# A mean over rows, loaded in blocks of 256 rows: which partition receives which pair of rows

## The chip, the cores and the metric

The kernel runs on one core of one Trainium2 chip. The metric is the device time of one execution, in microseconds. The kernel before takes 1244.01 us, the median of three runs (1243.89, 1244.03 and 1244.01).

## The reference: what is computed

The input is `x`, fp32, of shape (64, 256, 8192): 16,384 rows of 8,192 numbers, 536.9 MB. The output is the mean of each row.

```python
def reference(x):
    return np.mean(x, axis=2)
```

## The kernel before

Everything is bound together by one large stream of loads from HBM into the on-chip buffer memory (SBUF, 128 partitions).

**The blocks.** The 16,384 rows are cut into 64 lots of 256 rows. The first 63 of them (`NB` = 63) are the blocks. A block is 8 MiB. Each of the 128 partitions receives one *pair* of rows, that is two rows that lie behind each other in HBM, 64 KB in one piece. In the kernel before, partition p gets pair p of the block (`blocks`, L39), so a block is read as one contiguous stretch, cut into 128 pieces.

**The buffers and the load queue.** There are three buffers of 8 MiB (`bufs`, `NBUF` = 3). All loads are issued by SP, in order, on one hardware queue, and the chip's DMA engines, sixteen for this core, carry them out. The first block is issued as two loads (8 KB of each partition at L114, the other 56 KB at L115), so that a first semaphore comes early; blocks 1 and 2 follow at L117. Then a loop (L118 to L123) runs over the other 60 blocks: SP waits at L120 until the buffer is free, and issues the next load into it at L121. The loop picks its block with a register as index.

**The sums.** VectorE (DVE) waits for each block and adds up both rows of all partitions with one instruction (L163, `tensor_reduce` of 128 x 16384). Its result goes to two columns of `res`, and the instruction's end frees the buffer. The last three blocks are handled at L173 and, the very last, in two halves by the helper at L145.

**The last 256 rows** are loaded in smaller pieces so that little is left to do after the last byte: 128 rows, one per partition (`one`, L125), three groups of 32 rows with a quarter row per partition (L127), and a fourth group in four narrow pieces (L129). DVE and ScalarE (ACT) add them up as they land.

**The way out.** `res` holds, in partition p and columns 2g and 2g + 1, the sums of the two rows of partition p of block g. TensorE multiplies `res` by a diagonal matrix that holds 1/8192 (L226), which turns it: `turn[0]` and `turn[1]` have a block per partition and the 128 pairs as columns. ACT copies the two into `turned`, one into the even columns and one into the odd (L207), so that a partition of `turned` holds the 256 means of a block in the order of the output. SP stores that with one DMA (L133). The last 256 means go through `row` and leave by L135.

## Time and profile before

| | |
|---|---|
| median of three runs | 1244.01 us |
| the profiled execution's own time | 1243.67 us |
| its span, first to last instruction | 1242.4 us |
| DVE busy | 1085.4 us (87%) |
| DMA queue, share of sixteen engines' span | 99.8% |
| moved | 536.94 MB, 432 GB/s over the span |
| one sum of a block (L163) | 17.22 us, 60 times |
| issue of a block's load by SP (L121) | 0.33 us, 60 times |
| from issue to landing of a block's load | 40.3 us, two loads in the queue |

The page of the profile gives busy time by engine, then the span in forty slices, the DMA queue, the chain of work that ended last, and the groups of instructions. "L163" is line 163 of the kernel. The share of the DMA queue says how much of the sixteen engines' time was taken by packets. Each packet here is one contiguous piece of a load, as large as 64 KB.

### The profile page before, as it was taken

Reading aid. Unit: us, or ns where it says so; the run is one execution under the profiler, and the core shown is the slowest. Engines: PE = TensorE matmul, PEld = TensorE weight load, DVE = VectorE, ACT = ScalarE, POOL = GpSimd, SP = SyncE. Lnnn points to the kernel's source line nnn. Section 1 sums busy time; section 2 is a strip of 40 time slices with the busy share of each in tenths; the row PEclk is TensorE's granted clock in tenths of the full one; section 3 lists DMA queues with packets and bytes.
Section 4 is the critical chain, followed back from the end, with each engine's and each line's share of the span. In section 5 each row is a group of like instructions: output and inputs, shape, how many; then the busy total and the mean of one; then the engine's idle time right before and its main releaser. Section 6 shows DMA issues by size and latency. Waiting matters only on the chain. (4 is left out here: it accounts for less than half of the span.)

```text
span 1242.4 us, 656 instructions
## 1 busy us (share of the span) xinstructions
PE 3.3 (0%) x20; PEld 1.4 (0%) x20; DVE 1085.4 (87%) x78; ACT 3.7 (0%) x8; POOL 1.6 (0%) x11
## 2 busy tenths in 40 slices
PE   0000000000000000000000000000000000000001
PEld 0000000000000000000000000000000000000000
DVE  2898988989889898898898988989889898898988
ACT  0000000000000000000000000000000000000000
POOL 0000000000000000000000000000000000000000
DMA  9999999999999999999999999999999999999998
GB/s 405 439 439 439 439 411 433 439 439 439 439 439 420 424 439 439 439 439 439 426 418 439 439 439 439 439 426 418 439 439 439 439 439 433 414 437 439 439 439 373
DMA packets 10442, 536.94 MB, mean 432 GB/s; under 512 B 1162, under 2 KB 1482, under 8 KB 1738
## 3 DMA queue, kind: packets, MB, share of 16 engines
q1 hardware_dynamic: 10442, 536.94, 99.8%
HBM read 536.87 MB, written 0.07 MB: 432 GB/s over the span
## 5 line engine op out<-in xcount | busy, mean ns | idle before, releaser
L163 DVE TENSOR_REDUCE res<-buf 128x16384 f32 x60 | 1033.2, 17220 | 146.9 <-DVEq L162 146.9
L173 DVE TENSOR_REDUCE res<-buf 128x2 f32<-128x16384 f32 x2 | 34.4, 17221 | 4.0 <-DMA buf<-in_x_dram 4.0
L145 DVE CUSTOM_DVE_ANT_0 buf<-buf 128x4096 f32<-128x4096 f32 (+2 forms) x7 | 17.2, 2485 | 4.2 <-DMA buf<-in_x_dram 4.2
L226 PE MATMUL turn<-diag,res 128*63 128x128 f32 x4 | 1.1, 428 | 1229.6 <-DVE res L145 1229.6
L207 ACT ACTIVATE turned<-turn 63x128 f32<-63x128 f32 x2 | 0.6, 281 | 1228.4 <-PE turn L226 1228.3
L226 PEld LDWEIGHTS turn<-diag,res 128*63 128x63 f32 x4 | 0.7, 217 | 1229.6 <-issue 1229.6
L235 PE MATMUL psum<-sel,part 128*1 128x32 f32 x14 | 1.6, 225 | 3.9 <-DVE part L145 3.1
L215 ACT ACTIVATE buf<-buf 128x896 f32<-128x896 f32 (+1 forms) x2 | 1.4, 709 | 7.9 <-DMA buf<-in_x_dram 7.8
L207 ACT ACT_TABLE_LOAD x1 | 1.3, 1283 | 0.7 <-PEq L262 0.7
L90 POOL TENSOR_SCALAR_AFFINE_SELECT sel<-sel 128x32 f32<-128x32 f32 x4 | 0.9, 213 | 0.7 <-POOL sel L87 0.2
L196 DVE TENSOR_REDUCE part<-buf 128x1 f32<-128x256 f32 x1 | 0.4, 419 | 0.3 <-DMA buf<-in_x_dram 0.3
L235 PEld LDWEIGHTS psum<-sel,part 128*1 128x1 f32 x14 | 0.6, 80 | 5.3 <-DVE part L145 3.9
L230 PE MATMUL psum<-diag,res 128*1 128x128 f32 x2 | 0.6, 394 | 4.1 <-DVE res L145 4.1
L200 DVE COPY row<-psum 1x32 f32<-1x32 f32 x1 | 0.2, 178 | 0.4 <-PE psum L235 0.4
L215 ACT ACTIVATION_READ_ACCUMULATOR buf<-buf 128x1 f32 x2 | 0.4, 186 | 0.0
L217 ACT ACTIVATE row<-psum 1x224 f32<-1x224 f32 x1 | 0.3, 330 | 0.0
L145 DVE DVE_READ_ACCUMULATOR2_ANT part<- 128x1 f32 x4 | 0.3, 81 | 0.0
L101 POOL TENSOR_SCALAR_AFFINE_SELECT diag<-diag 128x128 f32<-128x128 f32 x1 | 0.3, 295 | 0.1
L145 DVE DVE_READ_ACCUMULATOR2_ANT res<- 128x1 f32 x3 | 0.2, 83 | 0.0
L99 POOL MEMSET diag<- 128x128 f32 x1 | 0.2, 206 | 0.0
L87 POOL MEMSET sel<- 128x32 f32 x1 | 0.1, 125 | 0.3 <-POOLq L262 0.3
L262 POOL MEMSET const-bfloat16-1.0<- 128x1 bf16 x1 | 0.1, 102 | 0.0
(4 smaller groups left out, 0.4 us busy)
## 6 DMA issues: line engine op xcount, KB each, us to landing
buf<-in_x_dram SPq DMA_DIRECT2D x1, 7168.0 KB, 21.2
buf<-in_x_dram SPq DMA_DIRECT2D x4, 1024.0 KB, 34.1
buf<-in_x_dram SPq DMA_DIRECT2D x1, 4096.0 KB, 31.1
buf<-in_x_dram SPq DMA_DIRECT2D x62, 40.3
buf<-in_x_dram SPq DMA_DIRECT2D x1, 448.0 KB, 37.7
buf<-in_x_dram SPq DMA_DIRECT2D x1, 288.0 KB, 37.9
buf<-in_x_dram SPq DMA_DIRECT2D x1, 160.0 KB, 37.9
buf<-in_x_dram SPq DMA_DIRECT2D x1, 128.0 KB, 37.8
```

The lines of the kernel that those rows point to most:

```text
L90: eng.affine_select(out=sel[:], in_=sel[:], compare_op=mybir.AluOpType.not_equal, fill=inv, base=-q, pattern=[[-PER, G]], channel_multipli ...
L101: eng.affine_select(out=diag[:], in_=diag[:], compare_op=mybir.AluOpType.not_equal, fill=inv, base=0, pattern=[[-1, P]], channel_multiplier=1,
L145: eng.tensor_tensor_reduce(ap[:, 0:n], ap[:, 0:n], ap[:, n : 2 * n], scale=1.0, scalar=0.0, op0=ADD, op1=ADD, accum_out=to,).then_inc(done, 1)
L163: eng.tensor_reduce(early[:, bass.ds(i, 1), b, :], bufs[b][:].rearrange("p (j l) -> p j l", j=2), X, ADD,).then_inc(free_sems[b], 1)
L173: eng.tensor_reduce(res[:, 2 * g : 2 * g + 2], bufs[b][:].rearrange("p (j l) -> p j l", j=2), X, ADD,).then_inc(free_sems[0] if b == 0 els ...
L196: eng.tensor_reduce(part[:, PER + 2 : PER + 3], group(PER - 1)[:, a:z], X, ADD).then_inc(part_d, 1)
L207: eng.activation(turned[:, j : 2 * P : 2], turn[j][:, 0:P], COPY).then_inc(copy_sem, 1)
L215: eng.activation(ap, ap, COPY, accum_out=part[:, to : to + 1]).then_inc(part_a, 1)
L217: eng.activation(row[:, 0 : 2 * P - G], psum[0][:, 0 : 2 * P - G], COPY).then_inc(row_sem, 1)
L226: eng.matmul(turn[j][:, 0:P], res[:, j : 2 * NB : 2], diag[:], start=True, stop=True).then_inc(turn_sem, 1)
L230: eng.matmul(psum[0][:, 0:P], res[:, 2 * NB : 2 * NB + 1], diag[:], start=True, stop=True)
L235: return eng.matmul(dst, part[:, n : n + 1], sel[:], start=start, stop=stop)
```

## The change

The list of blocks is cut by another pattern. Within a block of 128 pairs, partition 8e + j now receives pair 16j + e, with e from 0 to 15 and j from 0 to 7. The pieces stay 64 KB, each contiguous, and a load still names all 128 partitions in order. What differs is the source side of the load: before, 128 steps of 64 KB; after, 16 outer steps (e) of 64 KB, and inside each 8 steps (j) of 1 MiB. The index of the block becomes the first dimension of the pattern. Since the partitions now hold the pairs in another order, ACT's copy into `turned` reads its 128 columns as 16 times 8 and writes them as 8 times 16, which puts the means back in the order of the output. The loads of the last 256 rows and everything on DVE and TensorE stay as they were.

```diff
+    RUN = 16
-    blocks = flat[0:M, :].rearrange("(g p j) l -> p g (j l)", p=P, j=2)
+    blocks = flat[0:M, :].rearrange("(g j e t) l -> g e j (t l)", g=NB, e=RUN, t=2)
...
-        later = blocks[:, NBUF:, :].rearrange("p (i b) w -> b p i w", b=NBUF)
-        eng.dma_start(bufs[0][:, 0:FIRST], blocks[:, 0, 0:FIRST]).then_inc(first_sem, 16)
-        eng.dma_start(bufs[0][:, FIRST:], blocks[:, 0, FIRST:]).then_inc(in_sems[0], 16)
+        later = blocks[NBUF:].rearrange("(i b) e j w -> b i e j w", b=NBUF)
+        eng.dma_start(bufs[0][:, 0:FIRST], blocks[0][:, :, 0:FIRST]).then_inc(first_sem, 16)
+        eng.dma_start(bufs[0][:, FIRST:], blocks[0][:, :, FIRST:]).then_inc(in_sems[0], 16)
         for b in range(1, NBUF):
-            eng.dma_start(bufs[b][:], blocks[:, b, :]).then_inc(in_sems[b], 16)
+            eng.dma_start(bufs[b][:], blocks[b]).then_inc(in_sems[b], 16)
         with eng.Fori(0, ROUNDS) as i:
             for b in range(NBUF):
                 eng.wait_ge(free_sems[b], 1).then_inc(free_sems[b], -1)
-                eng.dma_start(bufs[b][:], later[b][:, bass.ds(i, 1), :]).then_inc(
+                eng.dma_start(bufs[b][:], later[b][bass.ds(i, 1)]).then_inc(
                     in_sems[b], 16
                 )
...
-            eng.activation(turned[:, j : 2 * P : 2], turn[j][:, 0:P], COPY).then_inc(
-                copy_sem, 1
-            )
+            eng.activation(
+                turned[:, j : 2 * P : 2].rearrange("g (j e) -> g e j", e=RUN),
+                turn[j][:, 0:P].rearrange("g (e j) -> g e j", e=RUN),
+                COPY,
+            ).then_inc(copy_sem, 1)
```

## The prediction

> **What bounds the kernel now.** I read the page first: the share of the DMA queue, beside the busy share of the fullest engine.

> ```profile
> span 1242.4 us, 656 instructions
> PE 3.3 (0%) x20; PEld 1.4 (0%) x20; DVE 1085.4 (87%) x78; ACT 3.7 (0%) x8; POOL 1.6 (0%) x11
> ...
> DMA  9999999999999999999999999999999999999998
> ...
> q1 hardware_dynamic: 10442, 536.94, 99.8%
> ```

> The sixteen DMA engines are full from end to end; DVE has 13% to spare. The stretches view says the same without the start and the tail (columns: stretch, its length, busy time of PE, weight loads, DVE, ACT, POOL, clock, DMA share, GB/s):

> ```profile
> 31.00:620.00 589.00, 0.00 (x0) 0.00 (x0) 525.42 (x31) 0.00 (x0) 0.00 (x0) 1.00 1.00 434
> 620.00:1180.00 560.00, 0.00 (x0) 0.00 (x0) 499.25 (x29) 0.00 (x0) 0.00 (x0) 1.00 1.00 434
> ```

> 434 GB/s in both, with a DMA share of 1.00. Next the waits, of the engines and of SP's queue:

> ```profile
> DVE res L163 <- DVEq L162: 146.9, 60, 22.6
> ```

> ```profile
> SPq L120 <- SPq L120: 1140.5, 60, 37.1
> SPq L133 <- ACT turned L207: 28.1, 1, 28.1
> SPq L135 <- DVE row L200: 9.8, 1, 9.8
> ```

> DVE waits at every block (22.6 us for the first, then about 2.1 us each), so it follows the loads. SP waits about 19 us for each free buffer, and yet each load then stands 40.3 us between issue and landing, twice a block's time: a second load is always queued ahead of it.

> The trace's own record of single packets says what "full" means. Of 7,936 pieces of 64 KB, 7,485 took exactly 2,418 ns; the shortest took 2,415 ns and the mean is 2,419.0. That is 27.1 GB/s for an engine, and sixteen of them are the 434 GB/s above. Pieces of 32 KB take 1,213 ns and pieces of 8 KB 309 ns: from 32 to 64 KB, 32,768 bytes more for 1,205 ns, 27.2 GB/s again. So a piece moves at a fixed rate of its engine's path, no engine slows another, and nothing in it varies as a shared memory's answer would.

> **The change part by part.** The sum is made against the profiled execution's 1243.67 us (0.03% below the median 1244.01).

> *What it can save.* The aim is sixteen engines reading neighbours. If every piece fell to the shortest seen, that is 63 blocks x 8 pieces per engine x (2,419.0 - 2,415) ns = 2.0 us, 0.16%. The start holds no more: the 128 first pieces of 8 KB averaged 344 ns over a usual 309, 8 x 35 ns = 0.3 us per engine. Neighbouring reads are already in this trace: the three quarter-row groups (L127) read 1 MiB stretches with all sixteen engines in them, and their 384 pieces all took 309 ns, the price of that size. I take a gain of 0.

> *SP's issues.* 60 times L121, 0.33 us each, two loads at L117 and two for the first block, all with a source pattern of one dimension more. Bounds: unchanged, or twice as long, 0.33 us more each. SP waits 19 us ahead of each and the queue holds another load, so 0. For the first load there is no cover: it is issued at 0.75 us for 0.42 us, so at most 0.4 us. I take 0.

> *ACT's two copies* (L207), 281 ns each, written in steps of 32 numbers instead of 2. Bounds: same, or three times as long, 1.1 us more for both. They end at 1231.0, SP's store L133 follows (0.37 us), and SP then waits 9.8 us at L135 for `row`. Cost 0; without that cover, 1.1 us. ACT's next work, L215, waits 7.8 us for a landing behind them. TensorE, POOL and the loads of the last 256 rows issue what they did.

> *DVE's* sums are the same 60 x 17.22 us. They lie beside the loads as long as a load takes longer than 17.22 us.

> *How a load is cut among the engines.* This is the term that decides. A load names 128 partitions; its source had 128 outer steps and now has 16, with 8 inside. As I read it, the new pattern hands one outer step, and with it eight neighbouring partitions (8e to 8e + 7), to each engine. Whether the engine had those partitions before, the profile doesn't show, since it has no engine or partition for a packet. If before the engines were dealt partitions so that each had an entry to SBUF of its own, eight neighbours each may put two engines at one entry, at the same moment, while other entries stand idle. Bounds: nothing, if the 27.1 GB/s is the engine's own limit; and if it is the entry's, two engines share it and each piece takes 2 x 2,418 ns. The nearest rows for both ends are the piece itself and the block cadence: DVE's sums at L163 start at 22.6 us and, 59 blocks later, at 1162.9, so 19.33 us a block. I take the upper end. The rows that lean that way: the rate is the same for 8 KB pieces and 64 KB pieces, near ones and far ones, and all sixteen engines hold it within 0.1%, which is how sixteen separate, exactly full paths look. If it is a path's limit, sharing is paid in full.

> [...]

> *How long they meet.* [...] The packet record has the sixteen engines starting their first piece within 0.45 us of each other. All pairs must end for a block to end, so the pair with the smallest lead counts; I take 0.1 us, which is 0.2 us a block. Nothing in the trace makes a lead grow.

> The sum: 63 blocks x 19.33 us = 1217.8 us more, less 63 x 0.2 = 12.6 us: 1243.67 + 1217.8 - 12.6 = 2448.9. I predict 2449 us. DVE would then be busy 44% (1085.4 of 2449) and SP's waits twice as long.

> **The rivals.**

> *A. Not slower: the limit is in the engine, not at the entry.* Or the cut stays as it was. Then each piece keeps its 2,418 ns wherever it is written, 8 x 2.42 = 19.3 us a block, and the time is 1243.7 us with a bound of 2 us below. For it: the same uniform rate, which an engine's own limit explains as well. It decides as soon as a piece written beside its neighbour takes 2.42 us and not more. Against it: that the change touches the very shape by which the load is cut.

> *B. The pairs meet at first and drift apart.* [...] Then the first blocks take 38.7 us and later ones 19.3. With the crossing done on average halfway, the loss is half: 1243.7 + 609 = 1853 us; quick drift would give 1300, slow drift 2400. [...] Against it: pieces that agree to 1 ns in 2,418 point to a very even treatment of the engines.

> *C. HBM is slower for neighbours.* The engines are in step, 64 KB apart. The only slow pieces of the trace are those of the first load, 344 ns on average instead of 309. As a bound, 11% on the 1218 us of blocks, 134 us; a third of it gives about 1290 us. Against it stand the 384 pieces at 309 ns.

> *D. Faster by more than 0.2%.* It needs pieces below the shortest of 7,936, or the 2.2 us outside the packets.

> **How the numbers follow.** 0.2%, 2.5 us, is about what a measurement of this kernel can tell from no change. I give the forecast 0.40: the rows allow a limit of the path or of the engine, and of these the path with its full pairing is a little likelier, given that the shape by which the load is cut changes. B gets 0.27, the same limit with an uneven split. A gets 0.25, all of it within 0.2%. C gets 0.06 and D 0.02. So slower 0.40 + 0.27 + 0.06 = 0.73, same 0.25, faster 0.02. Leaving A out would leave more than 2 in 10 out, and so would leaving the forecast out; the range has to go from A's lower bound, 1243.7 - 2.0, to the full doubling without a lead, 1243.7 + 1217.8: 1242 to 2462. The forecast's own range is 2386 (a lead of 0.6 us, 76 us less) to 2462.

> **What would show it.** If the forecast holds: a DMA share still near 1.00 at about 217 GB/s; the loads of blocks land some 77 us after issue; DVE starts a sum every 38 to 39 us, waiting 21 us; the tail of `one` and the groups moves at today's rate, since those loads are cut as before. If B: GB/s climbing along the span from 217 to 434. If A: every row as it was, with L207 alone changed. If C: a few per cent in all slices alike. The prediction is wrong if a block lands in 19.3 us in the first slices, or if ACT's copies or SP's issues show up in the chain that ended last.

## The result and the profile after

The changed kernel takes 2575.61 us (median of six runs, 2572.72 to 2582.77); the kernel before, 1244.02 us in six runs. The ratio is 2.071, with a 95% interval of 2.068 to 2.074. The forecast was slower, at 2449 us with a range up to 2462; the way was right, the size too small by 127 us, and the time lies above the range. The profiled execution took 2572.72 us.

The page of the changed kernel: the engines' busy time, the DMA share and rate by slice, the queue.

```profile
span 2571.4 us, 656 instructions
...
PE 3.3 (0%) x20; PEld 1.4 (0%) x20; DVE 1085.4 (42%) x78; ACT 3.9 (0%) x8; POOL 1.6 (0%) x11
...
DMA  9999999999999999999999999999999999999999
GB/s 212 212 196 212 212 203 205 212 212 196 212 212 211 197 212 212 196 212 212 212 196 212 212 201 207 212 212 196 212 212 205 203 212 212 196 212 212 210 198 262
...
q1 hardware_dynamic: 10442, 536.94, 100.0%
```

The queue carries the same 10,442 packets and the same bytes, and the DMA engines are still full. DVE does the same 1085.4 us of work. Only the rate is halved, evenly over the whole span, until the last slice, where the last 256 rows are loaded as before the change. (That slices differ between 196 and 212 means little: sixteen engines start their 64 KB pieces within 0.60 us of each other and finish them nearly together, and a slice holds a whole number of such rounds.) The stretches view of the changed kernel (stretch, length, busy time of PE, weight loads, DVE, ACT, POOL, clock, DMA share, GB/s):

```profile
100.00:700.00 600.00, 0.00 (x0) 0.00 (x0) 251.85 (x16) 0.00 (x0) 0.00 (x0) 1.00 1.00 208
1900.00:2500.00 600.00, 0.00 (x0) 0.00 (x0) 258.30 (x15) 0.00 (x0) 0.00 (x0) 1.00 1.00 208
```

208 GB/s early and late, where it was 434. The waits of DVE, and then those of SP's queue:

```profile
DVE res L165 <- DVEq L164: 1413.0, 60, 43.6
```

```profile
SPq L122 <- SPq L122: 2393.2, 60, 57.4
SPq L135 <- ACT turned L209: 57.4, 1, 57.4
SPq L137 <- DVE row L202: 9.4, 1, 9.4
```

DVE's wait for blocks grows from 146.9 to 1413.0 us, and SP's for free buffers from 1140.5 to 2393.2. What the change added on the instruction side can be read from the views of the line L123 (the loads) and of the tile `turned` (ACT's copies):

```profile
L123 SPq DMA_DIRECT2D buf<-in_x_dram x60: 539/540/577, 61.1 to 2446.4; - x60
...
DMA to landing us min/median/max: 103.6/103.6/103.7
```

```profile
L209 ACT ACTIVATE turned<-turn x2: 388/389/390, 2559.7 to 2560.1; 63x128 f32<-63x128 f32 x2
```

An issue costs 540 ns in place of 333, a copy 389 in place of 281; both are covered, the one by SP's waits, the other by the 9.4 us that SP stands at L137 afterwards. The page's chain of the work that ended last does name L209:

```profile
DVE res L175 1%; DVE buf L147 0%; ACT buf L219 0%; PE turn L230 0%; PE psum L239 0%; ACT turned L209 0%; DVE row L202 0%; DVE res L165 0%; DVEq L165 0%; DVEq L162 0%; DVE res L147 0%
```

But the copy there (0.39 us) is followed by 7.3 us in which ACT waits for the data of its next work, so it did not set the end:

```profile
ACT buf L219 <- DMA buf<-in_x_dram: 7.3, 1, 7.3
```

The record of single packets says where the time is. Before, 7,936 pieces of 64 KB took 2,419 ns on average. After, each of them takes either about 4,925 ns (a quarter of them: every fourth round of sixteen pieces) or about 5,105 ns (the other three rounds), 5,062 on average. That is 2.04 and 2.11 times 2,418. No piece kept its old duration; the shortest took 4,916 ns.

### The profile page after: what moved, and what is told of

Its sections match the earlier page's. It is cut to its first block, busy times and chain, and to the rows that moved or that the text cites. A ratio compares the mean times of both kernels' runs of the same rounds, so it can differ in the third digit from the quotient of the medians.

```text
span 2571.4 us, 656 instructions
## 1 busy us (share of the span) xinstructions
PE 3.3 (0%) x20; PEld 1.4 (0%) x20; DVE 1085.4 (42%) x78; ACT 3.9 (0%) x8; POOL 1.6 (0%) x11
## 2 busy tenths in 40 slices
DMA packets 10442, 536.94 MB, mean 209 GB/s; under 512 B 1162, under 2 KB 1482, under 8 KB 1738
## 3 DMA queue, kind: packets, MB, share of 16 engines
q1 hardware_dynamic: 10442, 536.94, 100.0%
## 5 line engine op out<-in xcount | busy, mean ns | idle before, releaser
L165 DVE TENSOR_REDUCE res<-buf 128x16384 f32 x60 | 1033.2, 17220 | 1413.0 <-DVEq L164 1413.0
L147 DVE CUSTOM_DVE_ANT_0 buf<-buf 128x4096 f32<-128x4096 f32 (+2 forms) x7 | 17.2, 2485 | 25.0 <-DMA buf<-in_x_dram 25.0
L209 ACT ACTIVATE turned<-turn 63x128 f32<-63x128 f32 x2 | 0.8, 389 | 2557.7 <-PE turn L230 2557.7
## 6 DMA issues: line engine op xcount, KB each, us to landing
buf<-in_x_dram SPq DMA_DIRECT2D x62, 103.6
```

Of the source, the lines that this page charges most:

```text
L147: eng.tensor_tensor_reduce(ap[:, 0:n], ap[:, 0:n], ap[:, n : 2 * n], scale=1.0, scalar=0.0, op0=ADD, op1=ADD, accum_out=to,).then_inc(done, 1)
L165: eng.tensor_reduce(early[:, bass.ds(i, 1), b, :], bufs[b][:].rearrange("p (j l) -> p j l", j=2), X, ADD,).then_inc(free_sems[b], 1)
L209: eng.activation(turned[:, j : 2 * P : 2].rearrange("g (j e) -> g e j", e=RUN), turn[j][:, 0:P].rearrange("g (e j) -> g e j", e=RUN), COPY ...
```

## The experiments

**Neighbours, in 32 steps.** The changed kernel with 32 runs of four partitions.

```diff
-    RUN = 16
+    RUN = 32
```

> The changed kernel with 32 outer steps in place of 16: partition 4e + j gets pair 32j + e, e from 0 to 31, j from 0 to 3. [...] Theory H (HBM is slow when sixteen engines read neighbours): about 2575 us. Theory C (a source with one dimension more makes every engine slow, wherever it writes): about 2575 us.

Measured: 1244.43 us (11 runs) against 1244.11 (15 runs), ratio 1.0003, interval 0.9994 to 1.0012. The stretches of this kernel:

```profile
31.00:620.00 589.00, 0.00 (x0) 0.00 (x0) 525.27 (x31) 0.00 (x0) 0.00 (x0) 1.00 1.00 434
620.00:1180.00 560.00, 0.00 (x0) 0.00 (x0) 499.13 (x30) 0.00 (x0) 0.00 (x0) 1.00 1.00 434
```

434 GB/s, as before the change, and the pieces are back at 2,418 ns. The source has two dimensions here too, and SP's issue costs 538 ns, nearly as in the changed kernel (540). So C falls, and neighbours that are read at a time neither gain nor cost anything that can be measured (at each step the 32 runs hold neighbouring pairs, as the 16 did).

**The cut without the neighbours.** Three blocks share 384 pairs of rows, and by S an engine reads eight of them that lie behind each other.

```diff
-    blocks = flat[0:M, :].rearrange("(g j e t) l -> g e j (t l)", g=NB, e=RUN, t=2)
+    blocks = flat[0:M, :].rearrange(
+        "(i e b j t) l -> i b e j (t l)", b=NBUF, e=RUN, j=P // RUN, t=2
+    )
...
-        later = blocks[NBUF:].rearrange("(i b) e j w -> b i e j w", b=NBUF)
+        later = blocks[1:].rearrange("i b e j w -> b i e j w")
...
```

> The cut of the changed kernel, 16 outer steps of 8 pairs, without the neighbours: three blocks are taken together, and partition 8e + j of block b of the three gets pair 24e + 8b + j, so an engine reads eight pairs that lie behind each other and the engines lie 1.5 MiB apart. The means are left in the order of loading. Theory S: 2575 us, since the partitions of an engine are the same as in the changed kernel. Theory H: 1244 us. Theory C: 2575 us.

Measured: 2578.25 us (4 runs), ratio 2.0694 (2.0654 to 2.0734). Its stretches:

```profile
100.00:1300.00 1200.00, 0.00 (x0) 0.00 (x0) 500.87 (x30) 0.00 (x0) 0.00 (x0) 1.00 1.00 207
1300.00:2500.00 1200.00, 0.00 (x0) 0.00 (x0) 516.60 (x30) 0.00 (x0) 0.00 (x0) 1.00 1.00 206
```

The whole loss without any neighbours: H falls. The loss belongs to the cut of 16 steps of eight partitions, whatever it reads.

**Eight, two and four steps.** The same line with 8, 2 and 4. The share of sixteen engines' time tells how many engines carry a load.

> The changed kernel with 8 outer steps of 16 partitions each. A load is then cut among eight engines at most. [...] Without any sharing, eight engines at 2.42 us a piece: 63 x 38.7 + 20 = 2457 us. Theory C: 5120 us. Theory H: between the two, since only eight engines read.

> [...] Theory C: every piece at 5.06 us, 20400 us. [...]

> The changed kernel with 4 outer steps of 32 partitions: four engines at most, engine 0 with partitions 0 to 31, engine 1 with 32 to 63, and so on. [...] Without sharing: 63 x 77.4 + 20 = 4895 us.

Measured, one run each: 5123.81 us with eight steps, 9778.49 with two, 5158.31 with four. The queue's row with eight, with two and with four steps:

```profile
q1 hardware_dynamic: 9930, 536.94, 50.6%
```

```profile
q1 hardware_dynamic: 9546, 536.94, 12.8%
```

```profile
q1 hardware_dynamic: 9674, 536.94, 25.6%
```

The shares are those of eight, two and four engines out of sixteen: in these three runs as many engines carry a load as its source has outer steps. Two engines take 2,418 ns a piece, so they don't disturb each other; 64 pieces for a block and 20 us for the rest are 63 x 154.8 + 20 = 9770 us, beside the 9778.49 measured. Eight engines take 5,068 ns a piece on average; 16 of them for a block are 63 x 81 + 20 = 5120 us, beside 5123.81; they bring 105 GB/s, a little less than four engines that don't disturb each other (109, below).

Four engines that met in every piece would need 32 pieces of 5.06 us for a block, 63 x 162 + 20 = 10220 us (an estimate). The run took half of that, and the rate by slice shows how:

```profile
GB/s 61 60 67 76 85 100 109 108 109 108 109 109 108 109 108 109 109 108 109 108 109 109 108 109 108 109 109 108 109 108 109 109 108 109 108 109 109 108 132 110
```

It starts at 60 GB/s, little above the 54 of two engines, and climbs within about 800 us to 109, twice that. The packet record fits one engine of each two that share pulling ahead of the other: the engines begin the 56 KB pieces of block 0 in two groups 1.1 us apart; a piece of the early group runs nearly undisturbed (2,585 ns; in the kernel before one of 56 KB took 2,116), its counterpart in the late group takes 3,809, and one piece of the late group shortens by some 180 ns each time it comes round (3,771, 3,591, 3,411, 3,232). From about 0.8 ms on the pieces take 2,418 ns. This is the prediction's rival B, in a kernel other than the one forecast.

**Out of step from the start.** To see whether the meeting itself is the cost, the leads were given instead of waited for. Block 0 is loaded in uneven parts, 17, 51 and 60 partitions (its means come out in another order); blocks 1 to 62 are loaded by the same instructions as with four steps.

```diff
-        eng.dma_start(bufs[0][:, 0:FIRST], blocks[0][:, :, 0:FIRST]).then_inc(first_sem, 16)
-        eng.dma_start(bufs[0][:, FIRST:], blocks[0][:, :, FIRST:]).then_inc(in_sems[0], 16)
+        whole = flat[0 : 2 * P, :].rearrange("(p t) l -> p (t l)", t=2)
+        eng.dma_start(bufs[0][0:17, :], whole[0:17, :]).then_inc(first_sem, 16)
+        eng.dma_start(bufs[0][17:68, :], whole[17:68, :]).then_inc(one_sem, 16)
+        eng.dma_start(bufs[0][68:P, :], whole[68:P, :]).then_inc(in_sems[0], 16)
...
```

> [...] Blocks 1 to 62 are loaded by the same instructions as with 4 outer steps. The means of block 0 come out in the order of its partitions. Theory S with leads that last: the two of a pair are never at partitions that share a way, 63 x 77.4 + 20 + about 30 for the uneven start = 4930 us. If a lead closes again, or if the cause is not that two engines meet: about 10250 us.

Measured in one run: 4969.39 us, where S with leads that last had 4930. Its rate by slice:

```profile
GB/s 109 107 109 108 109 108 109 108 109 109 108 109 108 109 108 109 108 109 109 108 109 108 109 108 109 108 109 109 108 109 108 109 108 109 108 109 109 108 138 60
```

The climb is gone: the same loads run at 107 to 109 GB/s from the second slice on, where they ran at 60 (the first slice still holds block 0, which lands at 129.7 us). Where data lies in HBM, the shape of the loads and the number of engines are the same; only the loads of block 0 differ, and with them, by S, the engines' places relative to each other, which no record shows.

**Fewer partitions to a load.** The kernel before, with each block's load cut into eight loads of 16 partitions, or four of 32 (the edit in the loop, for 16).

```diff
-                eng.dma_start(bufs[b][:], later[b][:, bass.ds(i, 1), :]).then_inc(
-                    in_sems[b], 16
-                )
+                for p in range(0, P, 16):
+                    eng.dma_start(
+                        bufs[b][p : p + 16, :], later[b][p : p + 16, bass.ds(i, 1), :]
+                    ).then_inc(in_sems[b], 16)
...
```

> The kernel before, its pairs in their old order, with each block's load cut into eight loads of 16 partitions, one piece for each engine. All sixteen engines then write 16 neighbouring partitions at a time. [...] Theory C: the source has one dimension, 1244 us. Theory H: sixteen neighbours are read at a time, about 2575 us.

> [...] If a pair costs over twice a piece wherever its two partitions lie: pieces of 5.06 us, 63 x 8 x 5.06 + 20 = 2570 us. [...]

Measured, one run each: 4714.34 us with sixteen, 2580.74 with thirty-two. The stretches with sixteen, then with thirty-two:

```profile
100.00:2300.00 2200.00, 0.00 (x0) 0.00 (x0) 499.37 (x29) 0.00 (x0) 0.00 (x0) 1.00 1.00 112
```

```profile
100.00:1300.00 1200.00, 0.00 (x0) 0.00 (x0) 499.47 (x30) 0.00 (x0) 0.00 (x0) 1.00 1.00 207
```

With sixteen partitions to a load a piece takes 9,315 ns, 3.85 times 2,418. With thirty-two, about 4,935 and 5,126 ns, 5,078 on average, close to the prices of the changed kernel (5,062): the extra 5% comes with this cut as well. C, which had 1244 us for the loads of sixteen, falls once more. So does any account by the order of reading, such as the changed kernel's steps of 1 MiB: both runs read the rows in their old order. The fewer partitions a load names here, the slower it is, at a DMA share of 1.00 each time: 434 GB/s with 128, 207 with thirty-two, 112 with sixteen. That agrees with S by the times alone; which partitions have a way in common, no record shows.

**The changed kernel, out of step.** The same test on the sixteen steps themselves; block 0 alone is loaded unevenly, which was meant to put engines one, two or four pieces ahead (`AHEAD` = 1, 2 or 4). In the last two runs DVE also leaves out half of its sums in the loop.

```diff
-        eng.dma_start(bufs[0][:, 0:FIRST], blocks[0][:, :, 0:FIRST]).then_inc(first_sem, 16)
-        eng.dma_start(bufs[0][:, FIRST:], blocks[0][:, :, FIRST:]).then_inc(in_sems[0], 16)
+        AHEAD = 1
+        rows4, rows12 = 8 * AHEAD, 24 * AHEAD
+        by4 = flat[0:rows4, :].rearrange("(j e t) l -> e j (t l)", e=4, t=2)
+        by12 = flat[rows4 : rows4 + rows12, :].rearrange("(j e t) l -> e j (t l)", e=12, t=2)
+        rest = flat[rows4 + rows12 : 2 * P, :].rearrange("(p t) l -> p (t l)", t=2)
+        eng.dma_start(bufs[0][0 : 4 * AHEAD, :], by4).then_inc(first_sem, 16)
+        eng.dma_start(bufs[0][4 * AHEAD : 16 * AHEAD, :], by12).then_inc(one_sem, 16)
+        eng.dma_start(bufs[0][16 * AHEAD : P, :], rest).then_inc(in_sems[0], 16)
...
```

```diff
-                    bufs[b][:].rearrange("p (j l) -> p j l", j=2),
+                    bufs[b][:, 0:L].rearrange("p (j l) -> p j l", j=2),
```

> The changed kernel, 16 outer steps, with block 0 alone loaded in another way: 4 partitions by four engines, 12 by twelve, 112 by all sixteen. [...] All later loads are those of the changed kernel; the means of block 0 come out in the order of its partitions. [...] If a lead of over 1 us grows, as it did with 4 outer steps: lower, down to some 1300 us. If the loss does not come from meeting: 2575 us.

> As with one piece ahead, with two pieces: 8 partitions by four engines, 24 by twelve, 96 by sixteen. [...] Leads that grow: lower, down to some 1300 us. No meeting: 2575 us.

> As with two pieces ahead, and DVE sums only the first row of each pair in the 60 blocks of its loop, which leaves out half of that work (8.6 us a block in place of 17.2), so that buffers come free earlier and an engine that is ahead finds its next load already queued. If what holds leads back is the queue running dry once blocks get shorter: below the run with two pieces ahead and whole sums. If the queue plays no part: the same time.

> As the run before, half of the sums left out, with four pieces: 16 partitions by four engines, 48 by twelve, 64 by sixteen. [...]

Measured, one run each: 2568.09 us with one piece, 2560.72 with two, 2565.18 with two and half of the sums, 1445.7 with four and half of the sums. The rate by slice in the last two:

```profile
GB/s 193 210 212 207 210 210 210 212 207 210 210 210 212 204 212 210 210 212 204 212 210 210 210 207 212 210 209 211 207 212 210 208 212 207 212 210 208 212 207 229
```

```profile
GB/s 181 131 289 345 347 363 361 365 370 368 367 359 378 378 385 378 378 394 390 399 407 414 408 407 407 421 407 421 419 421 417 412 421 407 410 430 419 425 272 202
```

The third run shows that half the sums do nothing by themselves with two pieces. In the fourth, the loads of blocks 1 to 62, each instruction as in the changed kernel, begin slowly and then run at 345 to 430 GB/s: the cut of 16 steps isn't slow in itself, it is slow, by S, when the engines go in step. (Four pieces with whole sums were not run, so whether the leads need the earlier free buffers is not known.)

The first three came out 7.5 to 15 us below the changed kernel's median. The packet record says why they don't test leads that stay. Block 0 itself pushed the engines about: its pieces took up to 9.2 us with one piece and, with those of the next block, up to 8.5 with two, near the 9.3 of a piece in loads of sixteen partitions. And from 96 us on, in the third block, no piece of the loop took less than 4,707, 4,728 and 4,840 ns in the three runs, so by S no engine had a way to itself for a whole piece; with four pieces ahead over half of the pieces from 105 us on took under 2,500 ns. So the intended leads weren't there when the loop ran. Whether leads of one or two pieces would last is not shown.

## Why the prediction was right and wrong

*What it can save: nothing.* Right. With 32 steps, which keep the neighbours and have pieces of 2,418 ns again, the ratio is 1.0003.

*SP's issues and ACT's copies: 0.* Right, and inside the bounds: 540 ns (333 to 666), 389 ns each (281 to 843), both covered by the waits that were named. One sign of being wrong did appear, a copy in the chain that ended last; as a wait of 7.3 us follows it there, the sign was badly chosen and not the term.

*How a load is cut: two engines at one entry, paid in full.* The runs agree with the mechanism: the cut is slow without neighbours (2.0694), fast with 32 steps of the same dimensions (1.0003), and, in blocks loaded by the very same instructions, slow in step and fast out of step (60 against 109 GB/s with four steps, 208 against 345 to 430 with sixteen). That two engines meet at a way is inferred from these times, since no record names an engine or a way, and which partitions would have one in common is not shown. (Of the rows that the prediction gave for it, one is read a little too well: 8 KB in 309 ns is 26.5 GB/s, not 27.1.)

*The price of sharing: 2 x 2,418 ns as the upper bound.* This is the step that failed: the price was put too low. A piece took 4,925 or 5,105 ns, 2.04 or 2.11 times 2,418. DVE's sums of the last blocks start 40.43 us apart, where the bound was 38.66: 63 x 1.77 = 111.5 us.

```profile
2469.15 17.22 DVE L175 TENSOR_REDUCE res<-buf 128x2 f32<-128x16384 f32 x1 [23.00 <-DMA buf<-in_x_dram]
2509.58 17.22 DVE L175 TENSOR_REDUCE res<-buf 128x2 f32<-128x16384 f32 x1 [23.21 <-DMA buf<-in_x_dram]
```

The bound rested on the idea that a shared way loses nothing; no row of before could show that, and an upper end worked out from perfect sharing is no upper end.

*How long they meet: 0.1 us of lead, 0.2 us a block saved.* Also too kind, by 12.6 us: no run shows that a lead of 0.1 us saves 0.2 us a block, and no piece of the changed kernel took less than 4,916 ns. The two together are 124 of the 127 us between forecast and median; the profiled execution itself is 2572.72, 3 us below the median. That no lead grows was right: the sixteen engines start their pieces within 0.60 us of each other in every round, from block 1 to the last.

*Rivals.* B, pairs drifting apart, didn't happen in the changed kernel (208 GB/s early and late) but did with four steps, where the loss of 77.4 us a block was halted after some 800 us. A and D are refuted by the piece times, its C (HBM, H above) by the cut without neighbours.

*What would show it.* DMA share near 1.00 and the tail at its old rate: so it was (the last block of 8 MiB lands 21.4 us ahead of the end, 21.7 before). 217 GB/s forecast, 208 measured. The landing was forecast at 77 us after issue and took 103.6. This forecast was wrong by its own figures: DVE now frees a buffer 17.2 us into the next block's 40.4, so a new load waits for the other 23.2 us of that block and for one whole load, and then takes 40.4 us itself, 104 us in all. Before, it was 2.1 us and two times 19.3; with 21.4 and two times 38.66 the forecast should have been 99 us.

## What to carry to other kernels

Before the order of a load is changed, look at how its access pattern is cut: where the outermost count of the source falls from 128 to 16 (32 cost nothing here), a load still uses all sixteen engines and shows a DMA share of 1.00, and yet may run at half the rate (208 GB/s in place of 434). A full DMA row tells that DMA engines are occupied, not how fast they move (1.00 here at 434, 208 and 112 GB/s); the GB/s beside it, and the time of one piece, tell the rest. Where one resource is said to be shared, twice the time is an estimate of its price and not a bound (2.04 to 2.11 times here): leave room above it.

## What had not been expected

Read by S, two engines at one way move 64 KB each in 5.06 us, 25.9 GB/s for the way; four, if that is what 3.85 times the time means in the loads of sixteen partitions (an estimate), move theirs in 9.315, 28.1 GB/s; one alone, 27.1. So two engines that share would lose 4.5% and four gain 3.8%. Why is open; loads of thirty-two partitions pay about the same as the cut in 16 steps (5.08 us). And engines that share stayed in step for the whole run with sixteen engines (2.5 ms, all starts within 0.60 us) and with eight (5.1 ms, within 0.80 us but for the tail), but parted within 0.8 ms with four, where they had begun 1.1 us apart. That the lead at the start decides is a guess: the runs with given leads on sixteen steps could not settle it.
